# Decode attention in float32 with two sequences on 64 columns each of TensorE's array

## The chip, the cores and the metric

The kernel runs on one core of a Trainium2 chip. The metric is the device time of one execution in microseconds (us), as the median of several runs. The core has TensorE (PE: matmuls; PEld is its weight load), VectorE (DVE), ScalarE (ACT), GpSimd (POOL) and the queues that issue transfers, of which SP and POOL matter here.

## The reference

One step of a hybrid decoder layer for a prompt of 1024 tokens and for 8 sample sequences of 8 new tokens each. The samples attend over a paged cache of 2048 past rows (16 pages of 128 rows per sequence) and their own new rows:

```python
def mla_attend(q_lat, q_rope, q_pos, ckv, krope, k_pos):
    s = jnp.einsum('bthc,bsc->bhts', q_lat, ckv) + jnp.einsum('bthr,bsr->bhts', q_rope, krope)
    s = s.astype(jnp.float32) * ATTN_SCALE
    mask = k_pos[None, :] <= q_pos[:, None]
    s = jnp.where(mask[None, None], s, -jnp.inf)
    p = jax.nn.softmax(s, axis=-1).astype(ckv.dtype)
    return jnp.einsum('bhts,bsc->bthc', p, ckv)
...
        past_ckv = cache_ckv[l][page_table].reshape(dec_b, past_len, KV_LORA)
        past_kr = cache_krope[l][page_table].reshape(dec_b, past_len, ROPE_DIM)
```

A query has 256 latent and 64 rotary numbers, there are 8 heads, so a sequence has 64 query rows (8 heads x 8 tokens). The output `o_lat` is multiplied by `w_uv` per head. Around this stand dense projections, prompt attention and an MLP, in float32 accuracy.

## The kernel before

Most products use TensorE's rounded float32 format (f32r). A value is split into a rounded part h and a remainder l (`split`, L77 and L78: a cast on ScalarE, a subtraction on VectorE), and a product is three matmuls: h by h, h by l, l by h.

The stage that the change touches lies between the low-rank projections and the prompt attention. It has two strands that share TensorE:

- `dense`: 40 gate and conv projections (`gate_tile`), each of 3 chunks of about 362 columns with 24 matmuls (`mm24`, L189 to L191), and 13 modulation blocks (`ada_mm`, L148). A modulation block is in plain float32: 8 matmuls, each on 32 of the array's 128 columns, four side by side. One plain float32 matmul leaves two records in the trace.
- `queries` and then `decode`: generators whose steps are put between dense tiles by `merge`, RQ and RD steps to one dense tile.

The order in which each engine works is fixed when the program is built, by priority in program order among what is expected to be ready: decode matmuls stand between the dense ones singly or in small groups, and an engine then works through its list in order.

`decode` takes the sequences in four pairs j, with s = 0, 1 in a pair. A pair's scores `Pp` have 128 rows: 64 for each sequence. For each sequence and each group g of two pages `load_k` gathers a tile (`kraw`, two gathers on GpSimd, L501), casts it and subtracts (`kh`, `kl`, L510 to L512). The weights hold the h and the l part of one sequence's 64 query rows side by side, so that one matmul fills 128 columns; `score5` makes five matmuls (L532 to L536) of 256 columns, and `score_add` (L419, L420) adds the two halves of the result. Then softmax (L583 to L588), transposes of the probabilities (`p_t`, L556, full width), and per group and sequence four matmuls with the value tile (`nraw` gathered, split to `nh` and `nl`; L612, L613). At the end `W_uv` is applied (L642, 64 columns of data, 48 matmuls).

Gathered tiles have three buffers each (BK, BV), and one tile is fetched ahead. `decode` has 149 steps: 1 + 4 x (16 + 1 + 1 + 16 + 2) + 4.

Of the kernel before, what the change touches and what calls it, by code (L numbers as in the profile page):

```python
# [14 lines left out]
F32 = mybir.dt.float32  # L15
# [8 lines left out]
P = 128  # L24
D = 1024
KT = D // P
TP = 1024
# [17 lines left out]
BK, BV = 3, 3  # L45
NB = 13
RQ, RD = 2.5, 3.8
# [6 lines left out]
def hybrid_step(ctx, tc, xT, cT, wada, cvec, win, wqbs, wqn, wqr, wuk, wuv, wukT, wo, w1, w2,  # L54
# [173 lines left out]
    kch = dc.tile([P, 2, NS], F32R, name="kch")  # L228
    kcl = dc.tile([P, 2, NS], F32R, name="kcl")
    krs = dc.tile([P, NS], F32R, name="krs")  # L230
    natn_h = dc.tile([P, CL], F32R, name="natn_h")
    natn_l = dc.tile([P, CL], F32R, name="natn_l")
# [148 lines left out]
    nc.vector.tensor_tensor(krs[64:], kr[64:, TP:], f(krs[64:]), ALU.subtract)  # L381
# [3 lines left out]
    split(kch, kcl, kv[:, :, TP:])  # L385
# [3 lines left out]
    nc.vector.memset(f(natn_h), 0.0)  # L389
    nc.vector.memset(f(natn_l), 0.0)  # L390
    split(natn_h[:64], natn_l[:64], pt[:64, :CL])
# [4 lines left out]
    QLt = dc.tile([P, 2, 4, 2, 2, 64], F32R, name="QLt", tag="QLt")  # L396
    QRt = dc.tile([P, 4, 2, 2, 64], F32R, name="QRt", tag="QRt")
# [10 lines left out]
    ptn = dc.tile([P, 4, 64], F32R, name="ptn")  # L408
    nc.vector.memset(f(ptn), 0.0)
    OLh = dc.tile([P, 2, NH, NSEQ, NTOK], F32R, name="OLh", tag="OLh")  # L410
    OLl = dc.tile([P, 2, NH, NSEQ, NTOK], F32R, name="OLl", tag="OLl")
# [14 lines left out]
    def queries():  # L426
# [13 lines left out]
        qd = qp.tile([64, NH, 2, 64], F32, name="qd")  # L440
# [8 lines left out]
        tt(qd[:, :, 0, 0:32], ta, tb, ALU.subtract)  # L449
# [4 lines left out]
        tt(qd[:, :, 0, 32:64], ta, tb, ALU.add)  # L454
        nc.vector.tensor_copy(qd[:, :, 1], qd[:, :, 0])

        def put(dst, ps):

            src = ps.rearrange("p (h j s t) -> p s j h t", h=NH, s=2, t=NTOK)
            for s in range(2):  # L460
                for j in range(4):
                    hd = dst[:, j, s, s].rearrange("p (h t) -> p h t", t=NTOK)
                    ld = dst[:, j, s, 1 - s].rearrange("p (h t) -> p h t", t=NTOK)
                    split(hd, ld, src[:, s, j])
# [22 lines left out]
        for h in range(NH):  # L487
            nc.tensor.transpose(pr[:, h * 64:(h + 1) * 64], qd[:, h].rearrange("p a d -> p (a d)"), ident[:64, :64])
        put(QRt, pr)
# [25 lines left out]
    def load_v(j, s, g):  # L515
        raw = ds.tile([P, PG, CL], F32, name="nraw", tag="nraw", bufs=BV)
        if s is None:
            nc.sync.dma_start(raw, wuv[j].rearrange("p (c n) -> p c n", c=2))
        else:
            for i in range(PG):  # L520
                gather(raw[:, i], ntab, (2 * j + s) * NPG + g * PG + i)
        nh = ds.tile([P, PG, CL], F32R, name="nh", tag="nh", bufs=2)
        nl = ds.tile([P, PG, CL], F32R, name="nl", tag="nl", bufs=2)
        split(nh, nl, raw)
        return nh, nl

    def q_of(j, s):
        a = [QLt[:, c, j, s].rearrange("p a n -> p (a n)") for c in range(2)]
        return a[0], a[1], QRt[:, j, s].rearrange("p a n -> p (a n)")

    def score5(o, q, k0h, k0l, k1h, k1l, kr_):
        nc.tensor.matmul(o, q[0], k0h, start=True, stop=False)  # L532
        nc.tensor.matmul(o, q[0], k0l, start=False, stop=False)
        nc.tensor.matmul(o, q[1], k1h, start=False, stop=False)
        nc.tensor.matmul(o, q[1], k1l, start=False, stop=False)
        nc.tensor.matmul(o, q[2], kr_, start=False, stop=True)  # L536

    def decode():
        klist = [(j, s, g) for j in range(4) for s in range(2) for g in range(NG_)]
        vlist = [(j, s, g) for j in range(4) for g in range(NG_) for s in range(2)]  # L540
        kq, vq = [], []

        def more_k():
            if klist:
                kq.append(load_k(*klist.pop(0)))

        def more_v():
            if vlist:
                vq.append(load_v(*vlist.pop(0)))
# [12 lines left out]

        more_k()
        yield
        for j in range(4):
            Pp = ds.tile([P, NEWK], F32, name="Pp", tag="Pp")
            for s in range(2):
                q = q_of(j, s)
                ps = aux("S")
                score5(ps[:, :NS], q, kch[:, 0], kcl[:, 0], kch[:, 1], kcl[:, 1], krs)  # L570
                score_add(Pp[:, PAST:], ps, s, NS)
                for g in range(NG_):
                    kh, kl = kq.pop(0)
# [7 lines left out]
            nc.vector.tensor_tensor(Pp[:, PAST:], Pp[:, PAST:], dm[:, j], ALU.add)  # L581
# [8 lines left out]
            os = [aux("o"), aux("o2")]  # L590
            pt = aux("tp")
            nc.tensor.transpose(pt[:64, :P], Pp[:, PAST:], ident)
            src = pt[:64, :P].rearrange("p (s n) -> p s n", s=2)
            nc.scalar.copy(ptn[:64, 0::3], src)
            nc.vector.tensor_tensor(ptn[:64, 1:3], src, f(ptn[:64, 0::3]), ALU.subtract)
            PTn = p_t(Pp, 0)
            yield
            for s in range(2):
                lt = ptn[:, 2 * s:2 * s + 2].rearrange("p a n -> p (a n)")
                nc.tensor.matmul(os[s][:, :CL], lt, natn_h, start=True, stop=False)  # L600
                nc.tensor.matmul(os[s][:, :CL], lt, natn_l, start=False, stop=False)
            for g in range(NG_):
                PT = PTn
                for s in range(2):
# [5 lines left out]
                    for i in range(PG):  # L610
# [6 lines left out]
            for s in range(2):  # L617
                score_add(O, os[s], s, CL)
            nc.vector.tensor_scalar(O, O, rc, None, ALU.mult)
# [4 lines left out]
            for c in range(2):  # L624
                src = pt[:, c * P:(c + 1) * P].rearrange("p (s h t) -> p h s t", s=2, h=NH)
                split(OLh[:, c, :, 2 * j:2 * j + 2], OLl[:, c, :, 2 * j:2 * j + 2], src)
            yield
        ws = [load_v(0, None, None)]
        for q in range(4):
            h, l = ws.pop()  # L630
            if q < 3:
                ws.append(load_v(q + 1, None, None))
            for hh in range(2):
                hd = 2 * q + hh
                ps = aux("o" if hh else "o2")
                i = 0
                for c in range(2):
                    w = slice(hh * P, hh * P + P)
                    oh = OLh[:, c, hd].rearrange("p b t -> p (b t)")
                    ol = OLl[:, c, hd].rearrange("p b t -> p (b t)")  # L640
# [1077 lines left out]
```

## Time and profile before

| | before |
|---|---|
| median of 3 runs | 1856.6 us (1855.48 to 1861.61) |
| the profiled execution | 1858.57 us |
| its span, first to last instruction | 1856.8 us |
| TensorE busy | 1791.2 us (96%) |
| VectorE, ScalarE, GpSimd busy | 1138.4, 891.0, 448.5 us |
| decode stage, 209 to 708 us | 499.0 us, TensorE busy 479.43 |

In the trace, L612 is line 612 of the kernel. A group of instructions is given as line, engine, operation, out<-in, rows * columns of the array, shape, count, then busy us and mean ns of one, then the engine's idle time before them and what ended it. In a timeline the first number is the start in us and the second the duration; durations of matmuls include their way through the array and overlap, so that distances between starts tell what one costs. "x8" is eight records merged into one row.

### The profile page before, as it was taken

What the parts mean: (1) busy time and instruction counts of PE and PEld (TensorE: products, weight loads), DVE (VectorE), ACT (ScalarE), POOL (GpSimd) and SP (SyncE); (2) the same over time, 40 slices, a digit from 0 to 9 for tenths busy, and PEclk for the clock granted to TensorE, in tenths of its full rate; (3) what the DMA queues carried; (4) which work ended last, traced back from release to release, by engine and by line L of the source; (5) the groups of instructions that cost most, each with busy time, mean ns of one, the idle gap of its engine ahead of it and who ended that gap; (6) DMA issues with size and microseconds to landing.
All of it is one profiled execution on the core that took longest, in us unless ns stands there. A gap on an engine that the chain in (4) does not pass through costs nothing.

```text
span 1856.8 us, 33160 instructions
## 1 busy us (share of the span) xinstructions
PE 1791.2 (96%) x12612; PEld 1714.6 (92%) x12612; DVE 1138.4 (61%) x2159; ACT 891.0 (48%) x1762; POOL 448.5 (24%) x448
## 2 busy tenths in 40 slices
PE   7999999999999999999999999999999999999997
PEld 4999899898998989889889899999999999999997
DVE  5573474554636443376876665977665657776874
ACT  5333343544434433266666645845555553434452
POOL 0110575647656341221210000013222200000000
PEclk9999999999999999999999999999999999999998
DMA  8235464545544344311211762556434479756761
GB/s 336 70 109 189 134 193 130 175 143 154 167 144 146 122 148 139 100 55 57 65 53 56 255 206 83 178 191 214 158 136 148 150 247 310 259 172 210 235 212 56
DMA packets 149024, 292.64 MB, mean 158 GB/s; under 512 B 22448, under 2 KB 56112, under 8 KB 148608
## 3 DMA queue, kind: packets, MB, share of 16 engines
q1 hardware_dynamic: 130464, 240.70, 39.5%
q0 software_dynamic: 14368, 42.03, 7.5%
q10 hardware_dynamic: 4032, 7.80, 1.1%
q8 instruction: 99, 1.62, 0.4%
q14 instruction: 61, 0.50, 0.1%
HBM read 230.69 MB, written 59.76 MB: 156 GB/s over the span
## 4 chain that ended last, share of the span: by engine, by line
PE 78%; DVE 6%; issue 6%; DMA 4%; ACT 3%; POOL 2%; another core or an unknown queue 1%; SPq 0%; POOLq 0%; ACTq 0%; DVEq 0%
PE mm L189 7%; PE mm L190 7%; PE mm L191 7%; PE mm L1267 6%; PE mm L1265 6%; PE mm L1266 6%; PE mm L1475 5%; PE mm L1476 5%; PE mm L1474 5%; POOL nraw L501 2%; DMA nraw<-in_ntab,pti 1%; PE tp L918 1%; PE mm L1152 1%; PE mm L1154 1%; PE mm L1153 1%
## 5 line engine op out<-in xcount | busy, mean ns | idle before, releaser
L189 PE MATMUL mm<-uh,wh 128*128 128x362 f32 (+2 forms) x1152 | 381.9, 334 | 3.3 <-issue 2.4
L191 PE MATMUL mm<-uh,wl 128*128 128x362 f32 (+2 forms) x1152 | 379.6, 330 | 3.1 <-issue 3.1
L190 PE MATMUL mm<-ul,wh 128*128 128x362 f32 (+2 forms) x1152 | 381.0, 331 | 1.6 <-issue 1.4
L189 PEld LDWEIGHTS mm<-uh,wh 128*128 128x128 f32 x1152 | 219.5, 191 | 12.2 <-issue 8.6
L190 PEld LDWEIGHTS mm<-ul,wh 128*128 128x128 f32 x1152 | 220.3, 191 | 5.0 <-issue 3.3
L191 PEld LDWEIGHTS mm<-uh,wl 128*128 128x128 f32 x1152 | 220.2, 191 | 4.6 <-issue 4.3
L1475 PE MATMUL mm<-g,fh 128*128 128x272 f32 x768 | 220.8, 288 | 0.1
L1476 PE MATMUL mm<-g,fl 128*128 128x272 f32 x768 | 220.5, 288 | 0.0
L1474 PE MATMUL mm<-g,fh 128*128 128x272 f32 x768 | 219.0, 288 | 1.1 <-ACT g L77 1.1
L501 POOL DMA_INDIRECT nraw<-in_ntab,pti x128 | 135.3, 1057 | 112.4 <-DVE nl L78 75.8
L501 POOL DMA_INDIRECT kraw<-in_ktab,pti x128 | 132.1, 1032 | 68.0 <-issue 35.5
L1474 PEld LDWEIGHTS mm<-g,fh 128*128 128x128 f32 x768 | 143.7, 188 | 1.4 <-ACT g L77 1.4
L1475 PEld LDWEIGHTS mm<-g,fh 128*128 128x128 f32 x768 | 144.6, 188 | 0.3 <-DVE g L78 0.3
L1476 PEld LDWEIGHTS mm<-g,fl 128*128 128x128 f32 x768 | 144.9, 189 | 0.0
L78 DVE TENSOR_TENSOR wl<-raw,wh 128x1024 fp32r<-128x1024 f32 (+1 forms) x66 | 80.6, 1222 | 62.7 <-ACT wh L77 51.6
L77 ACT CAST fh<-raw 128x512 fp32r<-128x512 f32 x112 | 68.8, 618 | 95.7 <-PE mm L1475 41.1
L78 DVE TENSOR_TENSOR nl<-nraw,nh 128x512 fp32r<-128x512 f32 x68 | 50.7, 755 | 98.0 <-ACT nh L77 60.0
L78 DVE TENSOR_TENSOR fl<-raw,fh 128x512 fp32r<-128x512 f32 x112 | 80.2, 720 | 49.2 <-ACT fh L77 49.0
L77 ACT CAST wh<-raw 128x1024 fp32r<-128x1024 f32 (+1 forms) x66 | 67.6, 1027 | 70.7 <-PE mm L190 36.4
L77 ACT CAST nh<-nraw 128x512 fp32r<-128x512 f32 x68 | 41.5, 620 | 108.8 <-DMA nraw<-in_ntab,pti 45.6
L78 DVE TENSOR_TENSOR g<-xl,g 128x544 fp32r<-128x544 f32 x112 | 79.4, 716 | 0.9 <-ACT g L77 0.9
L1320 ACT ACTIVATE xr<-xr 128x272 f32<-128x272 f32 x96 | 41.2, 431 | 70.1 <-DVE xr L1359 27.5
(633 smaller groups left out, 4978.9 us busy)
## 6 DMA issues: line engine op xcount, KB each, us to landing
raw<-in_w SPq DMA_DIRECT2D x220, 256.0 KB
raw<-in_win SPq DMA_DIRECT2D x46, 512.0 KB
xl<-h_t SPq DMA_DIRECT2D x64, 272.0 KB
aw<-in_wada SPq DMA_DIRECT2D x32, 512.0 KB
xl<-h_b SPq DMA_DIRECT2D x50, 272.0 KB
h_b<-xr SPq DMA_DIRECT2D x37, 272.0 KB
h_t<-xr SPq DMA_DIRECT2D x32, 272.0 KB
h_t<-xl SPq DMA_DIRECT2D x32, 272.0 KB
```

The lines of the kernel that those rows point to most:

```text
L77: nc.scalar.copy(h, src)
L78: (eng or nc.vector).tensor_tensor(l, src, f(h), ALU.subtract)
L189: nc.tensor.matmul(ps[:, :n], a, h, start=(k == 0), stop=False)
L190: nc.tensor.matmul(ps[:, :n], a, l, start=False, stop=False)
L191: nc.tensor.matmul(ps[:, :n], b, h, start=False, stop=(k == KT - 1))
L501: nc.gpsimd.indirect_dma_start(out=dst, out_offset=None, in_=tab, in_offset=bass.IndirectOffsetOnAxis(ap=pti[:, i:i + 1], axis=0))
L1265: nc.tensor.matmul(ps[:, :NC], a, h, start=(first and kk == 0), stop=False, skip_group_check=True)
L1266: nc.tensor.matmul(ps[:, :NC], a, l, start=False, stop=False, skip_group_check=True)
L1267: ins = nc.tensor.matmul(ps[:, :NC], a2, h, start=False, stop=(last and kk == 3), skip_group_check=True)
L1474: nc.tensor.matmul(o[:, :NC], a, h, start=z, stop=False)
L1475: nc.tensor.matmul(o[:, :NC], a, l, start=False, stop=False)
L1476: ins = nc.tensor.matmul(o[:, :NC], a2, h, start=False, stop=e)
```

## The change

Past keys, values, query weights and probabilities stay in plain float32; no cast, remainder or sum of halves is made. The two sequences of a pair are worked on together: the weights of sequence 0 stand on columns 0 to 63 of the array and those of sequence 1 on columns 64 to 127, as matmuls of their own with their own data, which write rows 0 to 63 and 64 to 127 of one accumulator. Scores of a group are 3 x 2 float32 matmuls of 256 columns, copied out by ScalarE in one piece; values are 2 x 2. `W_uv` is applied in plain float32 (16 matmuls); its four loads are issued together. The gathered tiles have six buffers each, four tiles are fetched ahead. `decode` has 85 steps (1 + 4 x 20 + 4), and RD goes from 3.8 to 2.2.

```diff
-BK, BV = 3, 3
+BK, BV = 6, 6
-RQ, RD = 2.5, 3.8
+RQ, RD = 2.5, 2.2
...
-    QLt = dc.tile([P, 2, 4, 2, 2, 64], F32R, name="QLt", tag="QLt")
-    QRt = dc.tile([P, 4, 2, 2, 64], F32R, name="QRt", tag="QRt")
+    QLt = dc.tile([P, 2, 4, 2, 64], F32, name="QLt", tag="QLt")
+    QRt = dc.tile([P, 4, 2, 64], F32, name="QRt", tag="QRt")
...
-    def load_k(j, s, g):
+    def load_k(j, g, s):
         raw = ds.tile([P, PG, 384], F32, name="kraw", tag="kraw", bufs=BK)
         for i in range(PG):
             gather(raw[:, i], ktab, (2 * j + s) * NPG + g * PG + i)
-        kh = ds.tile([P, PG, 384], F32R, name="kh", tag="kh", bufs=2)
-        kl = ds.tile([P, PG, 256], F32R, name="kl", tag="kl", bufs=2)
-        nc.scalar.copy(kh, raw)
-        nc.vector.tensor_tensor(kl, raw[:, :, :256], f(kh[:, :, :256]), ALU.subtract)
-        nc.vector.tensor_tensor(kh[64:, :, 256:], raw[64:, :, 256:], f(kh[64:, :, 256:]), ALU.subtract)
-        return kh, kl
+        return raw
...
-    def score5(o, q, k0h, k0l, k1h, k1l, kr_):
-        nc.tensor.matmul(o, q[0], k0h, start=True, stop=False)
-        nc.tensor.matmul(o, q[0], k0l, start=False, stop=False)
-        nc.tensor.matmul(o, q[1], k1h, start=False, stop=False)
-        nc.tensor.matmul(o, q[1], k1l, start=False, stop=False)
-        nc.tensor.matmul(o, q[2], kr_, start=False, stop=True)
+    def score3(ps, j, ks):
+        for c in range(3):
+            for s in range(2):
+                q = QLt[:, c, j, s] if c < 2 else QRt[:, j, s]
+                nc.tensor.matmul(ps[s * 64:s * 64 + 64], q, ks[s][c], start=(c == 0), stop=(c == 2))
...
-            PT = ds.tile([P, PG, 4, 64], F32R, name="PT", tag="PT", bufs=2)
-            src = pt[:, :PG * P].rearrange("p (g s n) -> p g s n", g=PG, s=2)
-            nc.scalar.copy(PT[:, :, 0::3], src)
-            nc.vector.tensor_tensor(PT[:, :, 1:3], src, f(PT[:, :, 0::3]), ALU.subtract)
+            PT = ds.tile([P, PG * P], F32, name="PT", tag="PT", bufs=3)
+            nc.scalar.copy(PT, pt[:, :PG * P])
...
-        more_k()
+        more(kq, klist, load_k, BK - 2)
         yield
...
-            for s in range(2):
-                q = q_of(j, s)
-                ps = aux("S")
-                score5(ps[:, :NS], q, kch[:, 0], kcl[:, 0], kch[:, 1], kcl[:, 1], krs)
-                score_add(Pp[:, PAST:], ps, s, NS)
-                for g in range(NG_):
-                    kh, kl = kq.pop(0)
-                    more_k()
-                    ps = rot("S", "o", "o2")
-                    o = ps[:, :PG * P].rearrange("p (g n) -> p g n", g=PG)
-                    score5(o, q, kh[:, :, 0:P], kl[:, :, 0:P], kh[:, :, P:2 * P], kl[:, :, P:2 * P], kh[:, :, 2 * P:])
-                    score_add(Pp[:, g * PG * P:(g + 1) * PG * P], ps, s, PG * P)
-                    yield
-            more_v()
+            ps = aux("S")
+            score3(ps[:, :NS], j, [[kcs[:, 0], kcs[:, 1], krs]] * 2)
+            nc.vector.tensor_tensor(Pp[:, PAST:], ps[:, :NS], dm[:, j], ALU.add)
+            for g in range(NG_):
+                k0, k1 = kq.pop(0), kq.pop(0)
+                more(kq, klist, load_k, 2)
+                ps = rot("S", "o", "o2")
+                o = ps[:, :PG * P].rearrange("p (g n) -> p g n", g=PG)
+                score3(o, j, [[k[:, :, c * P:(c + 1) * P] for c in range(3)] for k in (k0, k1)])
+                nc.scalar.copy(Pp[:, g * PG * P:(g + 1) * PG * P], ps[:, :PG * P])
+                if g >= NG_ - 2:
+                    more(vq, vlist, load_v, 2)
+                yield
...
-                for s in range(2):
-                    nh, nl = vq.pop(0)
-                    if (g, s) != (NG_ - 1, 1):
-                        more_v()
-                    if s == 0 and g + 1 < NG_:
-                        PTn = p_t(Pp, g + 1)
-                    for i in range(PG):
-                        lt = PT[:, i, 2 * s:2 * s + 2].rearrange("p a n -> p (a n)")
-                        nc.tensor.matmul(os[s][:, :CL], lt, nh[:, i], start=False, stop=False)
-                        nc.tensor.matmul(os[s][:, :CL], lt, nl[:, i], start=False,
-                                         stop=(g == NG_ - 1 and i == PG - 1))
-                    yield
+                PT, vs_ = PTn, (vq.pop(0), vq.pop(0))
+                if g < NG_ - 2:
+                    more(vq, vlist, load_v, 2)
+                if g + 1 < NG_:
+                    PTn = p_t(Pp, g + 1)
+                for i in range(PG):
+                    for s in range(2):
+                        nc.tensor.matmul(os[s * 64:s * 64 + 64, :CL], PT[:, i * P + s * 64:i * P + s * 64 + 64],
+                                         vs_[s][:, i], start=False, stop=(g == NG_ - 1 and i == PG - 1))
+                yield
...
+        def load_u(q):
+            raw = ds.tile([P, 2, CL], F32, name="uraw", tag="nraw", bufs=BV)
+            nc.sync.dma_start(raw, wuv[q].rearrange("p (c n) -> p c n", c=2))
+            return raw
+
+        ws = [load_u(q) for q in range(4)]
         for q in range(4):
...
-                    for a, b in ((h, oh), (h, ol), (l, oh)):
-                        nc.tensor.matmul(ps[:, :NS], a[:, c, w], b, start=(i == 0), stop=(i == 5))
-                        i += 1
+                    nc.tensor.matmul(ps[:, :NS], ws[q][:, c, hh * P:hh * P + P],
+                                     OL[:, c, hd].rearrange("p b t -> p (b t)"), start=(c == 0), stop=(c == 1))
```

The query side (`put`) copies to the new layout, and the new rows' keys and values (`kcs`, `krs`, `natn`), the probabilities of the new rows (`ptn`) and the outputs (`OL`) become plain float32 in the same way, each with one copy in place of a split.

## Rows read from the trace of the kernel before

**Rows 1.** Page, parts 1 and 2: busy us (share) xinstructions; the clock granted in 40 slices.

```profile
PE 1791.2 (96%) x12612; PEld 1714.6 (92%) x12612; DVE 1138.4 (61%) x2159; ACT 891.0 (48%) x1762; POOL 448.5 (24%) x448
...
PEclk9999999999999999999999999999999999999998
```

**Rows 2.** Decode stage: length, busy PE, PEld, DVE, ACT, POOL (instructions), clock, DMA, GB/s.

```profile
209.00:708.00 499.00, 479.43 (x3081) 453.64 (x3077) 255.41 (x461) 214.09 (x386) 281.42 (x283) 0.99 0.50 153
```

**Rows 3.** Groups of instructions by shape, TensorE, 209 to 708 us: decode matmuls after waits.

```profile
L612 PE MATMUL o<-nh,PT 128*128 128x256 f32 x128 | 36.9, 294 | 7.8 <-issue 5.6 <-ACT nh L77 2.2
...
L532 PE MATMUL o<-kh,QLt 128*128 128x256 f32 x42 | 12.7, 303 | 1.7 <-DVE O L420 0.9 <-issue 0.7
...
L536 PE MATMUL o<-kh,QRt 128*128 128x256 f32 x42 | 12.0, 286 | 0.4 <-issue 0.4
...
L532 PE MATMUL S<-kh,QLt 128*128 128x256 f32 x22 | 6.5, 295 | 2.1 <-issue 2.0
```

**Rows 4.** Timeline of TensorE: two dense matmuls (362 columns), then score matmuls (256).

```profile
606.68 0.32 PE L191 MATMUL mm<-uh,wl 128*128 128x362 f32 x1
606.85 0.33 PE L189 MATMUL mm<-uh,wh 128*128 128x362 f32 x1
607.01 0.28 PE L533 MATMUL o<-kl,QLt 128*128 128x256 f32 x1
607.13 0.28 PE L534 MATMUL o<-kh,QLt 128*128 128x256 f32 x1
```

**Rows 5.** Timeline of TensorE: rounded matmuls of 64 columns (with W_uv).

```profile
705.71 0.28 PE L642 MATMUL o<-OLl,nh 128*128 128x64 f32 x1
705.82 0.28 PE L642 MATMUL o<-OLh,nl 128*128 128x64 f32 x1
```

**Rows 6.** Timeline of TensorE, kernel start: float32 matmuls on 32 columns each.

```profile
23.91 0.64 PE L148 MATMUL S<-awh,cs 128*32 128x256 f32 x8
24.36 0.61 PE L148 MATMUL S<-awl,cs 128*32 128x256 f32 x8
24.80 0.61 PE L148 MATMUL tp<-awh,cs 128*32 128x256 f32 x8
```

**Rows 7.** Timeline of TensorE: one undisturbed modulation block between dense matmuls.

```profile
155.85 0.33 PE L191 MATMUL mm<-uh,wl 128*128 128x362 f32 x1
156.10 1.07 PE L148 MATMUL mm<-aw,cs 128*32 128x256 f32 x16
157.10 0.43 PE L189 MATMUL mm<-uh,wh 128*128 128x364 f32 x1
157.38 0.33 PE L190 MATMUL mm<-ul,wh 128*128 128x364 f32 x1
```

**Rows 8.** Timeline of TensorE: a modulation block broken up by score matmuls.

```profile
258.70 0.28 PE L536 MATMUL o<-kh,QRt 128*128 128x256 f32 x1
258.91 0.63 PE L148 MATMUL mm<-aw,cs 128*32 128x256 f32 x4
259.57 0.39 PE L532 MATMUL S<-kh,QLt 128*128 128x256 f32 x1
259.89 0.42 PE L148 MATMUL mm<-aw,cs 128*32 128x256 f32 x3
```

**Rows 9.** Gathers on GpSimd (timeline, group) and value and key splits, 190 to 710 us.

```profile
293.63 0.94 POOL L501 DMA_INDIRECT nraw<-in_ntab,pti  x1 [0.30 <-issue]
294.88 0.94 POOL L501 DMA_INDIRECT nraw<-in_ntab,pti  x1 [0.30 <-issue]
...
L501 POOL DMA_INDIRECT nraw<-in_ntab,pti x128 | 135.3, 1057 | 112.4 <-DVE nl L78 75.8 <-issue 31.2 <-DMA nraw<-in_ntab,pti 2.4
...
L77 ACT CAST nh<-nraw 128x512 fp32r<-128x512 f32 x68 | 41.5, 620 | 108.8 <-DMA nraw<-in_ntab,pti 45.6 <-remote 20.1 <-PE o L612 19.1
...
L78 DVE TENSOR_TENSOR nl<-nraw,nh 128x512 fp32r<-128x512 f32 x68 | 50.7, 755 | 98.0 <-ACT nh L77 60.0 <-remote 10.3 <-issue 8.2
L511 DVE TENSOR_TENSOR kl<-kraw,kh 128x512 fp32r<-128x512 f32 x64 | 45.4, 710 | 37.1 <-ACT kh L510 20.4 <-issue 9.5 <-DMA kraw<-in_ktab,pti 6.5
```

More of the change, by code (lines that the diff above doesn't have):

```diff
@@ L227, in hybrid_step @@
     qs = dc.tile([P, 3, P], F32R, name="qs")
[L228 to L232, printed above, removed]
+    kcs = dc.tile([P, 2, NS], F32, name="kcs")
+    krs = dc.tile([P, NS], F32, name="krs")
+    natn = dc.tile([P, CL], F32, name="natn")
     pa = scope()
@@ L384, in hybrid_step @@
     nc.sync.dma_start(ckvT, kv)
-    split(kch, kcl, kv[:, :, TP:])
+    nc.scalar.copy(kcs, kv[:, :, TP:])
     pt = aux("tp")
@@ L388, in hybrid_step @@
         nc.tensor.transpose(pt[:64, c * P:(c + 1) * P], kv[:, c, TP:], ident)
-    nc.vector.memset(f(natn_h), 0.0)
-    nc.vector.memset(f(natn_l), 0.0)
-    split(natn_h[:64], natn_l[:64], pt[:64, :CL])
+    nc.vector.memset(natn, 0.0)
+    nc.scalar.copy(natn[:64], pt[:64, :CL])
     px.close()
     pa.close()
-    QLt = dc.tile([P, 2, 4, 2, 2, 64], F32R, name="QLt", tag="QLt")
-    QRt = dc.tile([P, 4, 2, 2, 64], F32R, name="QRt", tag="QRt")
+    QLt = dc.tile([P, 2, 4, 2, 64], F32, name="QLt", tag="QLt")
+    QRt = dc.tile([P, 4, 2, 64], F32, name="QRt", tag="QRt")
+    nc.vector.memset(QRt[64:], 0.0)
     pti = dc.tile([P, NSEQ * NPG], I32, name="pti")
@@ L407, in hybrid_step @@
     nc.sync.dma_start(st, state)
[L408 to L411, printed above, removed]
+    ptn = dc.tile([P, P], F32, name="ptn")
+    nc.vector.memset(ptn, 0.0)
+    OL = dc.tile([P, 2, NH, NSEQ, NTOK], F32, name="OL", tag="OL")
     ms = wk.tile([P, NH, NS], F32, name="ms", bufs=1)
@@ L439, in queries @@
             score_add(qt[:, j * 256:(j + 1) * 256], ps, 0, 256)
-        qd = qp.tile([64, NH, 2, 64], F32, name="qd")
+        qd = qp.tile([64, NH, 64], F32, name="qd")
         x = qt[:, 1024:].rearrange("p (h s d) -> p h s d", h=NH, s=2)
@@ L453, in queries @@
         tt(tb, x[:, :, 0], sn, ALU.mult)
-        tt(qd[:, :, 0, 32:64], ta, tb, ALU.add)
-        nc.vector.tensor_copy(qd[:, :, 1], qd[:, :, 0])
+        tt(qd[:, :, 32:64], ta, tb, ALU.add)
         def put(dst, ps):
-            src = ps.rearrange("p (h j s t) -> p s j h t", h=NH, s=2, t=NTOK)
-            for s in range(2):
[L461 to L464, printed above, removed]
+            src = ps.rearrange("p (h j s t) -> p j s h t", h=NH, s=2, t=NTOK)
+            for j in range(4):
+                nc.scalar.copy(dst[:, j].rearrange("p s (h t) -> p s h t", t=NTOK), src[:, j])
         pn = aux("tp")
@@ L487, in queries @@
         for h in range(NH):
-            nc.tensor.transpose(pr[:, h * 64:(h + 1) * 64], qd[:, h].rearrange("p a d -> p (a d)"), ident[:64, :64])
-        put(QRt, pr)
+            nc.tensor.transpose(pr[:64, h * 64:(h + 1) * 64], qd[:, h], ident[:64, :64])
+        put(QRt[:64], pr[:64])
         yield
@@ L538, in decode, with load_v @@
+    def load_v(j, g, s):
+        raw = ds.tile([P, PG, CL], F32, name="nraw", tag="nraw", bufs=BV)
+        for i in range(PG):
+            gather(raw[:, i], ntab, (2 * j + s) * NPG + g * PG + i)
+        return raw
[4 more added lines that the diff above has]
+                nc.tensor.matmul(ps[s * 64:s * 64 + 64], q, ks[s][c], start=(c == 0), stop=(c == 2))
     def decode():
-        klist = [(j, s, g) for j in range(4) for s in range(2) for g in range(NG_)]
@@ L540, in decode, with more @@
-        vlist = [(j, s, g) for j in range(4) for g in range(NG_) for s in range(2)]
+        klist = [(j, g, s) for j in range(4) for g in range(NG_) for s in range(2)]
+        vlist = list(klist)
         kq, vq = [], []
[L543 to L549, printed above, removed]
+        def more(q, lst, load, n):
+            for _ in range(n):
+                if lst:
+                    q.append(load(*lst.pop(0)))
@@ L598, in decode @@
             for s in range(2):
[L599 to L601 removed]
+                r = slice(s * 64, s * 64 + 64)
+                nc.tensor.matmul(os[r, :CL], ptn[:, r], natn, start=True, stop=False)
             for g in range(NG_):
[L603 to L615 removed]
+                PT, vs_ = PTn, (vq.pop(0), vq.pop(0))
[3 more added lines that the diff above has]
+                    PTn = p_t(Pp, g + 1)
+                for i in range(PG):
+                    for s in range(2):
+                        nc.tensor.matmul(os[s * 64:s * 64 + 64, :CL], PT[:, i * P + s * 64:i * P + s * 64 + 64],
+                                         vs_[s][:, i], start=False, stop=(g == NG_ - 1 and i == PG - 1))
+                yield
             O = ds.tile([P, CL], F32, name="O", tag="O")
[L617 to L619 removed]
+            nc.vector.tensor_scalar(O, os[:, :CL], rc, None, ALU.mult)
             yield
```

33 lines of the change are left out of this document (5 added, 28 removed).

## Prediction

> **What bounds the kernel now.** I read the page's busy shares first, then busy time by stage, then TensorE's groups of instructions inside the decode stage, and last TensorE's and GpSimd's timelines there. TensorE is busy for 96% of the span, at nearly full clock (2.4 GHz) in all its slices [rows 1]. The change touches one stage, from the first score matmul at 209 us to the last W_uv matmul at 708 us. In these 499.0 us TensorE is busy 479.4, VectorE 255.4, ScalarE 214.1 and GpSimd 281.4 [rows 2]: only TensorE is near its limit, and dense projections stand ready to fill its gaps. So work that VectorE and ScalarE lose is worth only what it takes out of TensorE's waits. Of the 19.6 us in which TensorE is idle there, 12.0 stand in front of decode matmuls [rows 3]: 7.8 before L612, the first product with a value tile, and 4.2 before score matmuls (1.7, 2.1 and 0.4). The reader should see that this 12.0 is nearly all that a relief of the other engines can bring. Two matmuls that follow each other at once hide some 0.2 us of such a wait in their modelled ends, so with about ten waits I bound it by 14.
>
> **The change part by part: TensorE's own work.** Times go from start to start, since the printed durations overlap. A rounded (f32r) matmul of 256 columns takes 0.12 us, a dense one of 362 0.165 [rows 4]; f32r of only 64 columns takes 0.11, hardly less [rows 5]. Removed are:
> - scores of old keys: 64 tiles x 5 = 320 x 0.12 = 38.4 us
> - values: 64 x 4 = 256 x 0.12 = 30.7; the new values 16 x 0.12 = 1.9
> - 64 columns: 40 score matmuls on new keys and 48 with W_uv, 88 x 0.11 = 9.7
>
> Together 80.7 us. What comes instead is float32, which the trace has in one place with a column split: the modulation matmuls of L148, on 32 columns of the array each. Eight of its records (four matmuls, two records each) start every 0.44 us [rows 6]: the four run at the same time, each record a wave of 0.22 us, twice what 256 columns cost in f32r. Where the order of work left only two of those matmuls together, their four records again took about two waves (0.66 us from their start to the next instruction, the way back included) and not four [rows 8]. So I cost a pair of 64-column matmuls at two waves of 0.22 us:
> - scores: 32 groups x 3 pairs x 2 = 192 waves = 42.2 us
> - values: 32 x 2 pairs x 2 = 128 waves = 28.2; new values 8 waves = 1.8
> - new keys: 24 waves of 64 columns. No row has these; between a quarter of 0.22 (0.055) and the 0.11 of [rows 5], I take 0.08: 1.9
> - W_uv: 16 unsplit matmuls, 32 records of 64 columns between the same bounds; their weights are the full 128 columns, so 0.09: 2.9
>
> Together 77.0, or 3.7 us less; the bounds of the last two move it by 1.5 either way. Three products at f32r are thus hardly dearer than one float32 product on half the array; the packing wins nothing by itself.
>
> On overlap the Trainium skill, page "TensorE: Matmul & The Clock Gate", Part 3 (Packing small matmuls), measures 2.38x for three column tiles, not 3x. By that efficiency (0.79) an estimate for the 328 waves of 256 columns is 91 us in place of 72.2, and the sum below rises by 19. The waves of [rows 6] do not show such a loss, so the sum goes by the rows.
>
> **The price of changing the split.** Around an undisturbed L148 block, from the dense matmul before it (155.85) to the second one after it (157.38), 1.53 us pass [rows 7]. Two dense matmuls (0.33) and four waves (0.88) leave 0.32 us: TensorE runs empty before the first narrow matmul, and weights for the full array are loaded in the open after the last. The broken block gives more: from 258.70 to 258.91 0.09 too much, and 0.66 - 0.44 = 0.22 on the way back; the full-width matmul after it then holds the next narrow one 0.20 longer than its 0.12, of which I put half (0.10) to the way back. That is 0.41 [rows 8]. Before, no decode matmul paid this; now each run of them between full-width work does. The 32 value steps have full-width transposes (L556) between them, so each pays. The 32 score groups pay once per run: a dense tile is 72 matmuls x 0.165 = 11.9 us and 2.2 steps stand between two such tiles, so groups often come in twos, sometimes alone: 16 to 32 runs, I take 20. 52 x 0.35 = 18.2 us; from 48 x 0.32 = 15.4 to 64 x 0.41 = 26.2.
>
> **What the waits give back.** A value tile now comes off the gather and is used; before, a cast and a subtraction stood between (0.62 and 0.75 us, 68 times [rows 9]). More matters that GpSimd waited 75.8 us to refill value tiles until VectorE had let go of one of three [rows 9]. Six buffers and two groups fetched ahead end that. The 256 gathers stay; at 1.25 us from start to start [rows 9] they need 320 us of 499, 5.0 us for the four of one step against 499 / 85 = 5.9 us a step. In the last two score steps of each pair of sequences there are eight gathers, 10 us, which the steps without gathers (softmax, output) make up for. So I take the 7.8 us of the value side as gone and half of the 4.2 on the score side (2.1), since those are also waits for other engines: 9.9. Bounds: 0, if the steps now wait for landings instead, and 14.
>
> **Split pairs.** A score group now waits for two tiles, in order. If the first is in and the second isn't when the order is fixed, the halves are issued apart: six waves more and one more change of split, 6 x 0.22 + 0.35 = 1.7 us (values 4 x 0.22 + 0.35 = 1.2). If the second tile is late only on the chip, every dense matmul behind it in TensorE's queue waits too. Two groups ahead cover it: I allow 2 of 64, 2.9 us; bounds 0 and 16 groups (23).
>
> **Costed at nothing.** VectorE loses the subtractions (kl 45.4 and nl 50.7 us alone [rows 9]), ScalarE the casts; TensorE's dense work covered them, and where it did not, the 12.0 us of waits are their price. ScalarE gains 32 score copies of 128x256, of the size of the copies it loses; three score banks take turns, so the next group does not wait for them. Merging stays: 149 steps / 3.8 = 39 dense tiles, 85 / 2.2 = 39. The four W_uv loads go to SP's queue at once; a weight load behind them is covered by two tiles already loaded, and would cost its landing if not. Gathers keep their order on GpSimd's queue, behind the gate products (L685) as before.
>
> **Sum.** -3.7 + 18.2 - 9.9 + 2.9 = +7.5 us on the profiled execution's 1858.6, so 1866.1. The median shown is 2.0 lower; so 1864.
>
> **The rivals.**
> - *Faster.* All 14 us of waits go, no pair splits, and steps come so tightly that the split changes at most 32 times: -3.7 + 32 x 0.32 - 14 = -7.5, 1849. It decides at 38 changes; below, it is faster by 0.3%. For it: the waits are in one place with one cause. Against: the transposes alone ask for 32, and L148 blocks and dense tiles lie between.
> - *No change.* The waits go altogether and the price of 50 changes just eats them: -3.7 + 17.5 - 14 = -0.2, 1856.
> - *Pairs come apart* in a quarter of the groups: 23 in place of 2.9, +27.6, 1884. For it: in f32r a first score matmul was often issued alone. Against: the deeper buffers.
> - *The two halves overlap only in part*, which no row of 64 columns excludes: each 0.01 us on a wave costs 3.3 us; at 0.28 it is +27, 1884 (the skill's efficiency, above, comes out there), wholly in series 1936.
>
> **How the numbers follow.** 0.3% (5.6 us) is what a measurement here can tell from no change. The small loss has 0.37, no change 0.30, faster 0.20, pairs apart 0.09, part overlap 0.04. So faster 0.20, same 0.30, slower 0.50. The predicted time is the small loss, 1864, whose own range is 1858 to 1874 by the bounds of the change price and half the waits. The range, 1848 to 1886, takes in the faster case and pairs apart; it leaves out series and the far ends.
>
> **What would show it.** Right: waves of two 64-column records 0.22 us apart, some 50 entries with about 0.1 us before and 0.2 after them, idle time before value matmuls near nothing, nl and kl gone from VectorE, GpSimd no longer waiting for VectorE. Wrong: fewer than 38 changes, or no gap at them; runs of six records on one half alone; TensorE idle before score groups by more than 4 us; records of the two halves starting 0.22 us apart from each other with nothing beside them.

## The result, and the profile after

The changed kernel takes 1906.8 us (median of 4 runs, 1903.8 to 1909.7), the kernel before beside it 1859.1: a ratio of 1.0268, 95% interval 1.0241 to 1.0296. The forecast was a small loss, 1864 us, in a range of 1848 to 1886. One thing must be known to read every number below: the kernels were run in seven groups, each on one chip, and in two of them (this first pair, and the fifth of the later groups) the kernel before takes 1858 to 1859 us, in the other five 1830 to 1832; so each run is compared with the kernel before of its own group. One execution of the changed kernel with plain loads took 6478 us, at a granted clock of 0.39, and is left out of its numbers.

The page after, busy times and granted clock:

```profile
PE 1821.6 (96%) x12668; PEld 1683.8 (89%) x12668; DVE 967.9 (51%) x1811; ACT 785.0 (41%) x1570; POOL 427.3 (22%) x448
...
PEclk9999898899999999999999999999999999999999
```

The windows view of the stretch of [rows 2]:

```profile
209.00:708.00 499.00, 466.35 (x2817) 381.19 (x2816) 77.75 (x120) 99.05 (x180) 263.44 (x283) 0.95 0.46 142
```

VectorE's load there falls from 255.4 to 77.8 us and ScalarE's from 214.1 to 99.1, as forecast, and nothing comes of it: in the same 499 us TensorE is idle for 32.7 us in place of 19.6, and its clock is down to 0.95. The groups of instructions say where it is idle (last column: idle time before the group, and what ended it):

```profile
L189 PE MATMUL mm<-uh,wh 128*128 128x362 f32 (+1 forms) x623 | 212.1, 340 | 6.0 <-issue 6.0
...
L576 PE MATMUL o<-nraw,PT 128*64 128x256 f32 x256 | 45.0, 401 | 2.2 <-issue 2.1
L513 PE MATMUL o<-kraw,QLt 128*64 128x256 f32 x168 | 31.8, 402 | 5.3 <-issue 5.3
L513 PE MATMUL o<-kraw,QRt 128*64 128x256 f32 x84 | 20.0, 412 | 7.9 <-issue 7.9
```

Nearly all of it is "issue", time for which the profile shows no wait, and dense matmuls, which need nothing of the decode, have it too. The timeline of TensorE and GpSimd inside such a stretch:

```profile
230.16 0.95 POOL L493 DMA_INDIRECT kraw<-in_ktab,pti  x1 [0.30 <-issue]
...
231.41 0.94 POOL L493 DMA_INDIRECT kraw<-in_ktab,pti  x1 [0.30 <-issue]
231.75 0.29 PEld L191 LDWEIGHTS mm<-uh,wl 128*128 128x128 f32 x1 [1.92 <-issue]
232.47 0.46 PE L191 MATMUL mm<-uh,wl 128*128 128x362 f32 x1 [1.52 <-issue]
232.66 0.95 POOL L493 DMA_INDIRECT kraw<-in_ktab,pti  x1 [0.30 <-issue]
233.16 0.29 PEld L189 LDWEIGHTS mm<-uh,wh 128*128 128x128 f32 x1 [1.11 <-issue]
```

TensorE issues one instruction, weight load or matmul, every 0.70 us (231.75, 232.47, 233.16), full-width matmuls included, while GpSimd issues its gathers at an even 1.25 us. By the starts of TensorE's records there are seven such episodes in the decode stage (219 to 240 us is the longest), in which about 41 us are lost. Each begins 9 to 17 us into a run of ten or more gathers without a pause (starts at most 1.7 us apart) and ends within some us of the run's end. The granted clock falls behind them. Windows at the longest one, with the clock as third number from the end:

```profile
210.00:219.00 9.00, 9.00 (x49) 6.50 (x48) 0.54 (x1) 0.00 (x0) 6.76 (x8) 1.00 0.69 226
219.00:240.00 21.00, 6.98 (x17) 2.68 (x15) 0.00 (x0) 0.37 (x1) 13.15 (x14) 0.61 0.37 106
...
219.00:222.00 3.00, 1.18 (x5) 0.19 (x3) 0.00 (x0) 0.37 (x1) 2.39 (x3) 1.00 0.42 109
225.00:240.00 15.00, 4.38 (x10) 2.34 (x10) 0.00 (x0) 0.00 (x0) 8.53 (x9) 0.50 0.36 105
```

Over the 21 us the clock is 0.61 as a mean of its two levels: in the first 3 us, with five matmul records for 49 in the 9 us before, it is still 1.00 (2.4 GHz), and from 225 us on it is 0.50 (1.2 GHz). So the lower clock does not bring on the slow issue; it comes after it and adds to the loss: the dense matmuls behind this stretch start 0.30 us apart (240.62, 240.92 and 241.22) in place of 0.165. GpSimd's refills, in the group of value gathers from 190 to 720 us, now wait most for TensorE (44.6 of 91.3 us), no longer for VectorE [rows 9]:

```profile
L493 POOL DMA_INDIRECT nraw<-in_ntab,pti x128 | 125.9, 984 | 91.3 <-PE o L576 44.6 <-issue 32.2 <-remote 8.2
```

The first theory (A) was therefore: the deeper buffers let GpSimd issue gathers in long runs (27, 16, 14 and 12 in a row), and a long run slows TensorE. Rivals: the 64-column float32 matmuls themselves bring the gaps on (B); changes of split cost far more than forecast (C); and, from the second group on, the gaps belong to the chip (D).

### The profile page after: what moved, and what is told of

Read it like the earlier page. It is cut to its first block, busy times and chain, and to the rows that moved or that the text cites. A ratio compares the mean times of both kernels' runs of the same rounds, so it can differ in the third digit from the quotient of the medians.

```text
span 1902.0 us, 32345 instructions
## 1 busy us (share of the span) xinstructions
PE 1821.6 (96%) x12668; PEld 1683.8 (89%) x12668; DVE 967.9 (51%) x1811; ACT 785.0 (41%) x1570; POOL 427.3 (22%) x448
## 4 chain that ended last, share of the span: by engine, by line
PE 88%; DVE 3%; issue 3%; DMA 2%; ACT 2%; SPq 0%; POOL 0%; ACTq 0%; DVEq 0%; POOLq 0%
PE mm L189 10%; PE mm L190 10%; PE mm L191 10%; PE mm L1224 5%; PE mm L1226 5%; PE mm L1225 5%; PE mm L1434 5%; PE mm L1435 5%; PE mm L1433 5%; PE o L513 2%; PE o L576 2%; PE mm L1112 1%; PE mm L1113 1%; PE mm L811 1%; PE mm L1111 1%
## 5 line engine op out<-in xcount | busy, mean ns | idle before, releaser
L189 PEld LDWEIGHTS mm<-uh,wh 128*128 128x128 f32 x1152 | 220.3, 192 | 21.4 <-issue 18.2
L493 POOL DMA_INDIRECT nraw<-in_ntab,pti x128 | 125.9, 984 | 91.3 <-PE o L576 44.6
L493 POOL DMA_INDIRECT kraw<-in_ktab,pti x128 | 125.0, 977 | 90.3 <-issue 33.0
L642 ACT ACTIVATE sgx<-mm 128x362 f32<-128x362 f32 (+1 forms) x48 | 22.7, 473 | 123.5 <-PE mm L191 74.1
L77 ACT CAST g<-xl 128x544 fp32r<-128x544 f32 x112 | 71.0, 643 | 2.7 <-DMA xl<-h_b 2.7
L633 DVE TENSOR_TENSOR vb<-mm,cg 128x364 f32<-128x364 f32 (+2 forms) x24 | 12.3, 513 | 114.4 <-PE mm L191 57.8
```

Source lines behind the costliest of these rows:

```text
L77: nc.scalar.copy(h, src)
L189: nc.tensor.matmul(ps[:, :n], a, h, start=(k == 0), stop=False)
L493: nc.gpsimd.indirect_dma_start(out=dst, out_offset=None, in_=tab, in_offset=bass.IndirectOffsetOnAxis(ap=pti[:, i:i + 1], axis=0))
```

## The experiments

**Less fetched ahead.** Four buffers each, one group ahead:

```diff
-BK, BV = 6, 6
+BK, BV = 4, 4
-        more(kq, klist, load_k, BK - 2)
+        more(kq, klist, load_k, 2)
-                if g >= NG_ - 2:
+                if g == NG_ - 1:
-                if g < NG_ - 2:
+                if g < NG_ - 1:
```

> The changed kernel with four buffers for keys and four for values in place of six, and one group of each fetched ahead in place of two. Theory A (a run of a dozen or more gathers with no pause on GpSimd makes TensorE issue only one instruction per 0.7 us, and the deeper buffers made those runs): runs of gathers get shorter than about 12, the 41 us of slow issue fall below 10, time 1862 to 1878 us. Rival B (the 64-column float32 matmuls themselves bring on the slow issue): episodes stay at 30 to 45 us, 1895 to 1910 us. Rival C (changes between full and half array cost more than the forecast 0.35 us): no change beyond some us, 1895 to 1910 us, with few 0.7 us gaps involved.

Measured: 1863.4 us against 1832.4 for the kernel before in this group, ratio 1.0168 (1.0151 to 1.0186). The absolute time looks like A's, but by the ratio it fits none. Gathers still came in runs of 24 and 31 (counted as above), and there was no 0.7 us gap at all in the decode stage. A as first put falls.

**Plain loads in place of gathers**, in both kernels:

```diff
-        nc.gpsimd.indirect_dma_start(out=dst, out_offset=None, in_=tab,
-                                     in_offset=bass.IndirectOffsetOnAxis(ap=pti[:, i:i + 1], axis=0))
+        nc.sync.dma_start(dst, tab[i * P:i * P + P])
```

> The changed kernel with each gather through the page table replaced by a plain load of 128 consecutive rows issued by SyncE; the page table is left out, so other pages are read. Same bytes, same TensorE work, no gather on GpSimd. A: no 0.7 us episode in the decode stage, 1855 to 1870 us, some 40 us or more under the changed kernel. B and C: the slow stretches stay where the 64-column matmuls are, 1890 to 1910 us.

> The kernel before with the same replacement of gathers by plain loads on SyncE (page table left out). A: the 6 to 10 us of slow issue in the kernel before and the waits for gathers go, 1838 to 1852 us; the difference to the changed kernel with plain loads is then TensorE's own part of the change, forecast as -3.7 + 18.2 = +14.5 us less what waits remain. B and C: 1850 to 1860 us, the same as the kernel before.

> The changed kernel with plain loads, beside it. On a chip with gaps: A (gathers bring them on) says none here and about 1.000 of the kernel before or less; if the chip's TensorE is slow by itself, gaps at the same places. On a chip without gaps: 0.999 to 1.002 as before.

Measured: changed kernel 1834.1 us (ratio 1.0006, 0.9994 to 1.0017; again in the fourth group 1.0003, 0.9985 to 1.0021), kernel before 1817.4 (0.9918, 0.9901 to 0.9934). So without gathers the change costs 16.6 us, where the forecast's terms for TensorE alone (-3.7 and +18.2) come to +14.5; and gathers cost the kernel before 15.0 us. C is out: the changes do not cost far more than forecast.

**28 gathers beside full-width matmuls**, behind the decode stage of the kernel before, in rotating buffers, held back by a copy of the last W_uv result:

```diff
     merge(dn, decode(), RD)
+    next(dn)
+    for x in range(14):
+        raw = ds.tile([P, PG, 384], F32, name="xraw", tag="kraw", bufs=BK) if x % 2 == 0 else ds.tile([P, PG, CL], F32, name="yraw", tag="nraw", bufs=BV)
+        if x < 6:
+            nc.scalar.copy(raw[:, :, 0], ms[:, 7, :PG])
+        for i in range(PG):
+            gather(raw[:, i], ktab if x % 2 == 0 else ntab, x * PG + i)
+    next(dn)
     pds.close()
```

> The kernel before with 28 gathers more, in one run on GpSimd, placed behind the decode stage where TensorE does nothing but full-width projections; nothing reads what they fetch. A: after the first 10 to 13 of them (13 to 17 us) the projections' matmuls and weight loads go at one per 0.7 us until the run ends, some 15 to 20 us lost plus a stretch at half clock: 1871 to 1885 us. B: no episode, since no 64-column matmul is near: 1855 to 1862 us.

> The kernel before with 28 gathers more in one run beside full-width projections. On a chip with gaps: A says gaps in the projections after the first 10 to 13 of them, 15 us or more over the run on another chip; on a chip without gaps, 1847 us as before.

Measured: 1847.5 us, +15 (1.0080, 1.0059 to 1.0101), and 1848.0 in the fourth group, both without an episode of 0.7 us gaps. Windows of the second, a single execution, beside the extra gathers:

```profile
690.00:705.00 15.00, 15.00 (x94) 15.00 (x93) 6.11 (x9) 2.17 (x2) 11.47 (x12) 1.00 0.51 154
705.00:720.00 15.00, 15.00 (x92) 15.00 (x91) 2.08 (x5) 0.47 (x1) 11.91 (x14) 1.00 0.62 200
```

TensorE is busy throughout and at full clock; the time went after the run, 9.5 of it in one wait for ScalarE. Here 28 gathers in a row, with at most 0.3 us between them, do not slow TensorE. Two starts among them lie 1.8 and 2.2 us apart, so by the count used for A they are runs of 6, 10 and 12. Neither group shows the gaps in the decode stage either, so this says nothing of a group that has them.

**The changed kernel itself in other groups** (no edit):

> The changed kernel as it is, beside the kernel before on this chip. In the run with one group fetched ahead TensorE showed no 0.7 us gap although GpSimd issued 24 and 31 gathers without a pause, and the kernel before took 1832 us there against 1859. Theory A as first put (long runs of gathers slow TensorE, on any chip) says 40 us of 0.7 us gaps again and a ratio of 1.024 to 1.030. Rival D (the slow issue belongs to the chip of the first pair, not to the kernel) says under 5 us of such gaps and a ratio of 1.008 to 1.018: TensorE's own 16.6 us of the runs with plain loads, and up to 15 us of waits for gathers more or less.

> The changed kernel once more, on whatever chip this call gets, beside the kernel before. Rival D (the 0.7 us gaps belong to single chips): where the kernel before takes about 1832 us, no gaps and a ratio of 1.008 to 1.013; where it takes about 1857 us, gaps and a ratio of 1.024 to 1.030. Theory A without D: gaps on every chip.

> The changed kernel again, on the next chip. On three chips of four so far the kernel before took 1830 to 1832 us, and the changed one (on two of them) 1.010 of it without 0.7 us gaps; on the first, 1859 us and 1.027 with 41 us of gaps. D: gaps only if the kernel before takes about 1857 us here.

> The changed kernel on the next chip: 1.008 to 1.013 of the kernel before without 0.7 us gaps if that takes about 1831 us here, 1.024 to 1.030 with gaps if it takes about 1857 us.

Measured, in this order: 1849.8 us, ratio 1.0101 (1.0078 to 1.0124); 1849.5, 1.0101 (1.0073 to 1.0128); 1847.7, 1.0081 (1.0043 to 1.0118); 1901.7, 1.0230 (1.0208 to 1.0252). Only the last, where the kernel before took 1857.6 us, shows the gaps, at the first pair's places to within a few us; it ran on the same chip as the third, so D falls too. The same kernel on the same chip, by windows before, in and behind the decode stage, without gaps:

```profile
0.00:204.30 204.30, 188.61 (x1194) 171.38 (x1194) 106.69 (x189) 80.64 (x145) 26.07 (x36) 1.00 0.47 166
204.30:663.40 459.10, 456.00 (x2932) 385.10 (x2930) 87.02 (x129) 102.47 (x187) 268.63 (x287) 1.00 0.51 161
663.40:1845.90 1182.50, 1150.55 (x8547) 1116.38 (x8546) 776.86 (x1494) 602.21 (x1240) 134.20 (x126) 0.99 0.47 156
```

and with them:

```profile
0.00:204.40 204.40, 188.53 (x1194) 171.28 (x1194) 106.72 (x189) 80.66 (x145) 26.09 (x36) 1.00 0.47 166
204.40:720.30 515.90, 482.59 (x2933) 396.39 (x2930) 84.57 (x129) 102.41 (x187) 270.79 (x287) 0.95 0.46 143
720.30:1899.60 1179.30, 1148.98 (x8547) 1114.99 (x8545) 776.27 (x1494) 601.79 (x1240) 134.18 (x126) 0.99 0.48 157
```

The whole difference, 56.8 us for the same 2930 weight loads, lies in the one stage that has gathers; it holds the gaps and the work done at the lower clock. The kernel before loses 26 us (1857.6 against 1831.3). Its trace of the first pair shows the same slow issue, among dense matmuls:

```profile
227.76 0.19 PEld L191 LDWEIGHTS mm<-uh,wl 128*128 128x128 f32 x1 [0.20 <-issue]
228.46 0.32 PE L191 MATMUL mm<-uh,wl 128*128 128x364 f32 x1 [0.60 <-issue]
229.16 0.19 PEld L189 LDWEIGHTS mm<-uh,wh 128*128 128x128 f32 x1 [1.22 <-issue]
```

That kernel has no score or value matmul on 64 columns, so B is out too.

**Both in one kernel**: the changed kernel with plain loads, and the 28 gathers behind its decode stage.

> The changed kernel with plain loads in the decode stage (page table left out), and behind that stage one run of 28 gathers beside full-width projections, whose data nothing reads. Only two of the six groups of runs so far showed the 0.7 us gaps, the last of them on a chip that had shown none before. If this group shows them (kernel before at about 1857 us): gathers bring them on (A) means no gap in the decode stage, and 10 us or more of gaps in the projections from some 15 us after the first of the 28 gathers; TensorE slow by itself or by the 64-column matmuls (B, D) means gaps in the decode stage as in the changed kernel. If this group does not show them (kernel before at about 1831 us): no gaps at either place, and the time of the run with plain loads, 1834 us, plus what the gathers and copies add in the projections, some 10 to 15 us as in the run with 28 extra gathers.

Measured: 1848.6 us, 1.0094 (1.0065 to 1.0123), kernel before 1829.8: a group without gaps, and none at either place; 14.0 us are one wait for ScalarE behind the run. It does not tell the theories apart.

**The price and the number of changes of split.** What one run of narrow matmuls costs is read from start to start, from the dense matmul before it to the second one after it, less those two (0.33). Timelines of the changed kernel without gaps:

```profile
254.03 0.32 PE L191 MATMUL mm<-uh,wl 128*128 128x362 f32 x1
254.28 0.65 PE L513 MATMUL S<-kraw,QLt 128*64 128x256 f32 x2
254.86 0.43 PE L189 MATMUL mm<-uh,wh 128*128 128x362 f32 x1
255.13 0.33 PE L190 MATMUL mm<-ul,wh 128*128 128x362 f32 x1
...
457.84 0.32 PE L191 MATMUL mm<-uh,wl 128*128 128x362 f32 x1
458.09 1.08 PE L513 MATMUL o<-kraw,QLt 128*64 128x256 f32 x8
459.01 0.60 PE L513 MATMUL o<-kraw,QRt 128*64 128x256 f32 x4
459.44 1.03 PE L513 MATMUL o<-kraw,QLt 128*64 128x256 f32 x8
460.30 0.60 PE L513 MATMUL o<-kraw,QRt 128*64 128x256 f32 x4
460.83 0.43 PE L189 MATMUL mm<-uh,wh 128*128 128x364 f32 x1
461.10 0.32 PE L190 MATMUL mm<-ul,wh 128*128 128x364 f32 x1
```

One pair of matmuls, further on:

```profile
311.10 0.33 PE L189 MATMUL mm<-uh,wh 128*128 128x362 f32 x1
311.36 0.65 PE L576 MATMUL o<-nraw,PT 128*64 128x256 f32 x4
311.94 0.43 PE L190 MATMUL mm<-ul,wh 128*128 128x362 f32 x1
312.21 0.32 PE L191 MATMUL mm<-uh,wl 128*128 128x362 f32 x1
```

24 records take 461.10 - 457.84 - 0.33 = 2.93 us; runs of 12 take 1.65 and of 36 4.23, the same steps wherever dense matmuls stand on both sides and nothing is waited for. 12 records more are 1.29 us, six waves of 0.215, so 1.65 - 1.29 = 0.36 is the change there and back. The first lines are the case that the sum hardly had: one matmul alone (two records, one half), 255.13 - 254.03 - 0.33 = 0.77 us, as much as the pair (four records, 312.21 - 311.10 - 0.33 = 0.78); and the ten records left of its group take 1.64, as much as all twelve. Counted over the stage: 85 runs, 23 of them one matmul alone (12 with keys, 11 with values), in the changed kernel; 117 and 49 with one group ahead; 68 and 8 with plain loads. The order is fixed when the kernel is built, so it is the same in all groups.

Two tries to lower that number used four pages in a group (four buffers each, one group ahead):

```diff
-PG = 2
+PG = 4
-BK, BV = 6, 6
+BK, BV = 4, 4
...
-RQ, RD = 2.5, 2.2
+RQ, RD = 2.5, 4.4
```

> The changed kernel with four pages in a group in place of two (matmuls of 512 columns for scores, half as many groups, so half as many changes between full and half array), four buffers each and one group fetched ahead, a decode step for every 4.4 dense steps in place of 2.2. If a change of split costs the forecast 0.35 us, some 26 fewer save about 9 us against the changed kernel with one group ahead (ratio 1.017): 1.008 to 1.013. If changes cost nothing and the loss is in waits for gathers: 1.015 to 1.025, since a group then waits for twice as many gathers.

> The same with plain loads by SyncE in place of gathers (page table left out, so other pages are read). Against the changed kernel with plain loads (ratio 1.0006): by the price per change of 0.35 us 9 us less, ratio 0.994 to 0.997; if the 16.6 us that TensorE lost with plain loads are not in the changes but in the 64-column matmuls themselves, the same, 0.999 to 1.002.

Measured: 1861.4 us (1.0169, 1.0144 to 1.0195) and 1839.8 (1.0051, 1.0028 to 1.0073), both slower than meant: 4.4 was the wrong way, since there are half as many steps. With 1.1:

> The changed kernel with plain loads and groups of four pages again, now with 1.1 merge steps for a decode step, so that the decode stage lies over as much dense work as in the changed kernel (in the run before it lay over half as much, and the number of changes of split hardly fell, 59 against 68). Rows of the run with plain loads give about 0.29 us for a change and back (0.09 in, 0.20 out). If that is the price: some 25 changes fewer are 7 us less than with groups of two, ratio 0.996 to 0.998 against 1.0006. If waits for the larger groups take its place: 1.001 or more.

Measured: 1853.1 us (1.0124, 1.0101 to 1.0146). There are 44 runs, five of them one matmul alone, against 68 and eight. Taken from each start to the next, its decode and dense matmuls, transposes and modulation blocks take 689.2 us in place of 696.5 in the changed kernel with plain loads: 7 us less, 0.3 for each of the 24 runs. The total hides it: the decode stage now ends some 79 us later (727 us against 648), and a matmul of the next stage waits 25.6 us for ScalarE (the cast of its weights), where nothing was before.

**Pace and depth of fetch.** RD sets how much dense work lies between decode steps. In the changed kernel:

```diff
-RQ, RD = 2.5, 2.2
+RQ, RD = 2.5, 1.9
```

In the kernel before (the first line only in the run with values ahead, which also fetches a value tile three tiles before its cast):

```diff
-BK, BV = 3, 3
+BK, BV = 3, 4
...
-RQ, RD = 2.5, 3.8
+RQ, RD = 2.5, 3.3
```

> The changed kernel with a decode step for every 1.9 steps of the merge in place of 2.2, so that the decode stage is spread over some 46 dense items in place of 40 and the gathers over a longer time. If what the changed kernel loses beside TensorE's own work is waits for gathers (or slow issue under dense runs of them): 4 to 10 us under the changed kernel. If it is the changes of split alone: the same within 3 us, or some us more, since narrow groups then stand apart more often.

> The kernel before with 3.3 in place of 3.8 merge steps, the same stretch. The runs with plain loads put its cost of gathers at 15 us; if that is the wait of TensorE for the next buffers, more dense work between them hides 4 to 10 us of it: ratio 0.994 to 0.998. If it is not a wait but a slower TensorE beside gathers: 0.999 to 1.001.

> The kernel before with 3.3 in place of 3.8 merge steps, again (first 0.9978, interval 0.9965 to 0.9991). If more dense work between decode steps hides waits for gathers: 0.996 to 0.999 with an interval below 1. If the first was chance: an interval that holds 1.

> That, with a fourth value buffer and the values' pages fetched three tiles ahead of their casts in place of one, as the changed kernel does it. If the 2 us that TensorE still waits for values' casts and the changes of order around them go: 0.993 to 0.997. If fetching further ahead gives nothing back in the kernel before: the same as the run beside it, within 0.001.

Measured: changed kernel 1846.8 us, 1.0090 (1.0066 to 1.0115), too near the 1.0101 beside it to tell; kernel before 0.9978 (0.9965 to 0.9991) in a group without gaps and 0.9944 (0.9928 to 0.9959) in the one with them, 1848.3 us against 1857.6; with values fetched three tiles ahead 0.9962 (0.9944 to 0.9979). So the slower pace alone beats both kernels in both conditions; fetching further ahead adds nothing to it.

## Why the prediction was right or wrong

- **TensorE's own work and the change of split: right in the rows, the count too low.** Waves take 0.215 us (0.22 forecast), the halves overlap fully, and a change between dense matmuls costs 0.36 us (0.35). The Trainium skill (page "TensorE: Matmul & The Clock Gate", Part 3, Packing small matmuls) gives 2.38x for three column tiles. For two tiles these rows show next to no loss: a pair takes 0.78 us with its change, one matmul alone 0.77. The number of changes was too low: 62 runs besides the lone matmuls, +22.3, not 52, +18.2.
- **Own work, taken apart in the two kernels with plain loads.** They differ by 16.6. From start to start, the decode matmuls go from 81.6 to 89.1 us there, their transposes from 6.0 to 10.2, the dense matmuls from 575.9 to 580.4 and the modulation blocks from 20.2 to 16.8, since fewer of them are broken up; the other 4 us lie outside the stage and stay unexplained. The work removed was thus 81.6 (80.7 forecast), and the new work without changes is 75.8 (328 waves of 0.215, 3.3 for W_uv, 2.0 for new keys; 77.0 forecast): own work is -5.8 and not -3.7. The sum had no term for the 3.4 of the modulation blocks. What is left for 60 changes and 8 lone matmuls is 22, less than 60 x 0.36 + 8 x 0.77 = 27.8, so these prices are somewhat high where other work than dense matmuls stands beside a run.
- **Split pairs: the mechanism right, the size wrong.** "I allow 2 of 64, 2.9 us"; 23 matmuls are issued alone, 23 x 0.77 = 17.7 us, within the bounds given but six times the term. A single matmul comes off, not "six waves more". Two groups ahead do not cover it; they lower it from 49 (one group ahead) to 23.
- **Waits: near in size for the groups without gaps, not in place.** Gathers cost the kernel before 15.0 us; in the changed kernel TensorE's waits for them add up to 3.3. That is -11.7 against -9.9. But the forecast took 7.8 of it from in front of value matmuls and 2.1 from score matmuls. The nearest trace without gaps (the kernel before with 28 extra gathers behind the stage) is idle for 5.0 us in the stretch of [rows 2], 0.8 of it before L612 and 4.2 before score matmuls; from start to start, score matmuls take 6.1 us more there than with plain loads and value matmuls 2.3. So the larger part lay on the side that the forecast took for the smaller, and the nearness of the sum is in part luck. Check of the gathers' price in the changed kernel: 15 lone matmuls more than with plain loads (11.6), two other runs (0.7) and 3.3 make 15.6, and the two kernels are 15.3 apart in the fourth group. The same count overshoots with one group ahead: 35 for a measured 29.4.
- **The sum there**: from the measured 16.6 with plain loads, 16.6 + 15.6 - 15.0 = +17.2, measured +16.4 to +19.6 in three groups. The forecast was +7.5, so slower was right, by more than forecast and at the edge of the 1858 to 1874 given for that case. The largest miss is the split pairs, 17.7 for 2.9.
- **The step that failed for the recorded result** is "What the waits give back", and with it the line that costed the gathers at nothing for TensorE. I read the 12.0 us of idle time in [rows 3] as waits for casts and buffers, though 8.7 of it (5.6, 0.7, 0.4 and 2.0) stands there as "issue", a wait for nothing. In the kernel before with 28 extra gathers, in a group without gaps, the stretch of [rows 2] and the groups of [rows 3] read:

```profile
209.00:708.00 499.00, 493.97 (x3243) 476.67 (x3243) 261.11 (x471) 219.51 (x395) 307.77 (x302) 1.00 0.51 157
...
L612 PE MATMUL o<-nh,PT 128*128 128x256 f32 x128 | 36.1, 288 | 0.8 <-ACT nh L77 0.8
...
L532 PE MATMUL o<-kh,QLt 128*128 128x256 f32 x42 | 12.5, 299 | 1.7 <-DVE O L420 1.3 <-ACT kh L510 0.4
...
L532 PE MATMUL S<-kh,QLt 128*128 128x256 f32 x22 | 6.5, 295 | 2.5 <-ACT kh L510 2.5
```

TensorE is idle for 5.0 us in place of 19.6, and for 0.8 in place of 7.8 before L612: most of the idle time was the slow issue itself, in its smaller form. Fetching further ahead did not give it back; in the changed kernel it grew. The first pair's loss, 47.7 us, is the 17 of the other groups and some 30 that the gaps add, since they cost the kernel before 26 us and the changed one 52 to 57.
- **No rival had it.** Part overlap and pairs apart gave 1884, by other means. Of the signs named, one spoke: TensorE idle before score matmuls by more than 4 us (13.2 in the groups L513 above), all of it "issue".

What stays open is why two groups of seven show the gaps. It is not the chip (one showed both), not the run length alone (39 gathers in a row, without gaps, in the second group), not the pace of GpSimd (1.25 us from gather to gather with the gaps and without). That gathers are needed is argued from where the gaps lie, not shown: no kernel with plain loads met a group that has them. Not tried: one tile for the keys of both sequences and one for their values, so that no matmul can be issued alone. By the prices above the keys are worth up to 12 x 0.77 = 9.2 us and the values 11 x 0.77 = 8.5, together about the whole loss without gaps; this is an estimate.

## What to carry to other kernels

Idle time that a profile puts down to "issue" was here no wait that buffers could give back: find what else runs beside it before taking it as a gain. Where two matmuls are to share the array and wait for separate tiles, an order fixed at build time can issue one alone, at twice the price; one common condition for both should prevent it (not tried here). And a comparison in one group of runs can hold a condition of the machine that is worth more than the change; run the pair in another group before explaining it.

## What the runs showed of the hardware

- TensorE at one instruction per 0.70 us for up to 21 us beside an unbroken run of gathers, with no wait in the profile, in two groups of seven; the same kernel on the same chip took 1847.7 and 1901.7 us.
- In the longest such stretch the granted clock averaged 0.61, and 0.95 over the stage; the slow issue began while it was still 1.00.
- Float32 matmuls on two 64-column halves overlap fully: 0.215 us for each wave of 256 columns, in runs of 12, 24 and 36 records; the change to half the array and back costs 0.36 us between dense matmuls. One such matmul alone takes 0.77 us, a pair 0.78.
